# Weight sums of the up projection made in DRAM by accumulating DMA, and fifteen instead of thirteen pairs with seven products

## The chip, the cores and the metric

The kernel runs on one core of a Trainium2 chip. The metric is device time in microseconds: the median of several executions. TensorE (PE) multiplies, VectorE (DVE) and ScalarE (ACT) do elementwise work, GpSimd (POOL) does a few selects and issues the accumulating DMAs, SyncE (SP) issues the plain DMAs. Each engine runs its own instructions strictly in order; between engines there are semaphores. All DMAs run on 16 DMA engines.

## What is computed

One layer of an encoder on 512 tokens with 1024 channels, in float32: three token mixers on one normalised input (a forgetting attention, a gated delta rule, a stick-breaking attention), merged by gates and one output projection; then attention into 256 memory tokens; then a gated MLP. The change concerns the first matrix of the MLP, `w_up` (1024 x 5632):

```
x = x + mixed @ w_out
x = x + memory_cross_attention(rmsnorm(x, norm_xq), rmsnorm(mem, norm_mem), ...)

def conv_ffn(h, w_up, conv_w, conv_b, w_down):
    u = causal_dwconv(h @ w_up, conv_w) + conv_b
    a, b = jnp.split(u, 2, axis=-1)
    return (jax.nn.silu(a) * b) @ w_down

x = x + conv_ffn(rmsnorm(x, norm_ffn), w_up, ffn_conv, ffn_conv_b, w_down)
```

## The kernel before

**Units and splits.** All weights lie in DRAM as units of 128 x 1024 float32 (512 KB), in the order in which they are used. SP loads a unit into one of three buffers `wraw` (`load_unit`, L176). Each number is then split into a high part `whi`, rounded by ScalarE to TensorE's fast float32 format, and a low part `wlo`, the difference, by VectorE (`split_unit`, L181). Both have two buffers. A product of 128 x 512 takes three matmuls for each block of 128 channels: high x high, high x low, low x high (`mm3`, L208). A load is issued when VectorE has done with the unit three before it.

**The low part by DMA.** In the MLP most units get the low part in another way (`split_adding`, L288): ScalarE writes the negative of the rounded number into `alo`, and an accumulating DMA, issued by GpSimd, adds the unit from DRAM to it.

**Pairs.** The MLP has 22 pairs: unit 2m gives 128 columns of `a`, unit 2m + 1 the matching 128 of `b`. A plain pair multiplies both with all 512 tokens, 48 matmuls of 512 columns. A pair in `SEVEN` is made by Strassen's scheme in Winograd's form (`seven`, L297): the weights of the pair are a 2 x 2 array of blocks (a11, a12 in the first unit, a21, a22 in the second), the input another (channel half by token half), and seven products of half width take the place of eight. That is 84 matmuls of 256 columns. The sums of weight blocks s1 to s4 are made by VectorE (L305, L306, L314, L315) from the loaded units and split like units; the sums of input blocks, the token forms t14 and t23, are made once, behind pair 4 (`token_forms`, L1084). a1 and a22 get their low parts by accumulating DMA. Pairs 0 to 6, 15 and 21 are plain. The results lie in three PSUM banks px, py, pz, and five half-width operations of VectorE put them together. After each pair `gated` (L1111) applies the convolution and the gate.

**Stages and order.** The three mixers run first, in the order of the string `ORDER` (L30). Of its steps S3 projects the last stick-breaking head, s3 is that head's attention (its selects are GpSimd's last work for a long time), A, B, C are the gate projections, a, b, c the mixers' output projections, whose units appear as woa, wob, woc. Then come eight units of `wout` (wo0 to wo7) with four of the memory keys (mk) among them, the cross attention, the MLP's pairs, and the down projection. Inside this program order a scheduler fixes each engine's instruction order when the kernel is built; what it set ahead of time can be listed. The memory tokens are loaded as four tiles `mem_sb` (L374) when the mixing stage's buffers are free, and turned into `memh` and `meml` for the key projections.

Of the kernel before, what the change touches and what calls it, by code (L numbers as in the profile page):

```python
# [9 lines left out]
F32 = mybir.dt.float32  # L10
# [3 lines left out]
ALU = mybir.AluOpType  # L14
# [21 lines left out]
LOADS = (0, 1, 3, 2, 4, 5, 6, 7, 8, 9, 10)  # L36
# [45 lines left out]
def build(nc, tc, ctx, x_t, mem_t, w, cols_d, const_d, unit_d, out_t, dbg=None):  # L82
# [9 lines left out]
    def tiles_of(which, tag, bufs, shape=(T,)):  # L92
# [25 lines left out]
    spilled = ctx.enter_context(tc.tile_pool(name="spill", bufs=1, space=bass.MemoryType.DRAM)).tile(  # L118
        [P, KC, T], F32, tag="x3", name="x3_spill")

    def dense_ps(name):
        return pd.tile([P, T], F32, tag="d", name=name)
# [48 lines left out]
    ones_r = cp.tile([P, P], F32R, tag="ones_r", name="ones_r")  # L171


    last_mm = []

    def load_unit(u):  # L176
        raw = wp.tile([P, 1024], F32, tag="wraw", name=f"wraw{u}", bufs=WB[0])
        nc.sync.dma_start(raw, w[u])
        return raw

    def split_unit(u):  # L181
# [70 lines left out]
    def two(t):  # L252
        return t.rearrange("p (f n) -> p f n", f=2)

    def half_product(ps, unit, xs, behind=None):


        wh, wl = unit
        with ExitStack() as order:
            if behind is not None:  # L260
                order.enter_context(tc.issue_after(behind.ins))
            new = behind is None
            first = PE.matmul(ps, wh[:, block(0)], xs[0][0], start=new, stop=False, skip_group_check=not new)
            for i, (xh, xl) in enumerate(xs):
                if i:
                    PE.matmul(ps, wh[:, block(i)], xh, start=False, stop=False, skip_group_check=not new)  # L266
                PE.matmul(ps, wh[:, block(i)], xl, start=False, stop=False, skip_group_check=not new)  # L267
            for i, (xh, _) in enumerate(xs):
                PE.matmul(ps, wl[:, block(i)], xh, start=False, stop=i == 3, skip_group_check=not new)  # L269
        return first  # L270
# [17 lines left out]
    def split_adding(u, src, cols, name):  # L288

        lo = ahead(f"alo{name}", F32R)[:, :cols.stop - cols.start]  # L290
        hi = wp.tile([P, 1024], F32R, tag="whi", name=f"whi{name}", bufs=WB[1])[:, :cols.stop - cols.start]
        S.activation(lo, src, AF.Copy, scale=-1.0)  # L292
        G.dma_start(lo, w[u, :, cols], accum_op=ALU.add)  # L293
        S.activation(hi, src, AF.Copy)  # L294
        return hi, lo

    def seven(u, name, xs, forms, sums, outs, rest):  # L297


        a1, a2 = load_unit(u), load_unit(u + 1)  # L300
        (a11, a12), (a21, a22) = [(t[:, :T], t[:, T:]) for t in (a1, a2)]

        h1, l1 = split_adding(u, a1, slice(0, 2 * T), f"{u}")
        s1, s2, f12 = sums("12")
# [3 lines left out]
        if ADD_A22:  # L308
            h2, l2 = split_adding(u + 1, a22, slice(T, 2 * T), f"{u + 1}")
        else:  # L310
            h2, l2 = (wp.tile([P, 1024], F32R, tag=t, name=f"{t}{u + 1}", bufs=b) for t, b in (("whi", WB[1]), ("wlo", WB[2])))
            split_blocks(a22, h2[:, :T], l2[:, :T])
        s3, s4, f34 = sums("34")
# [5 lines left out]
        half_product(px[:, RIGHT], w5, forms[1], first)  # L319
        v = rest(f"v{name}")  # L320
        S.activation(v, px, AF.Copy)
        first_y = half_product(py[:, LEFT], (h2[:, :T], l2[:, :T]), forms[4])
        half_product(pz[:, LEFT], w6, forms[2])
        half_product(px[:, LEFT], (h1[:, T:], l1[:, T:]), halves_of(xs, 1, LEFT), first)
        half_product(py[:, RIGHT], w7, forms[3], first_y)
        half_product(px[:, RIGHT], w3, halves_of(xs, 1, RIGHT), first)
        u0, u1 = outs()
        V.tensor_tensor(u0[:, RIGHT], pz[:, LEFT], v[:, LEFT], ALU.add)
        V.tensor_tensor(u1[:, RIGHT], py[:, RIGHT], u0[:, RIGHT], ALU.add)
        V.scalar_tensor_tensor(u1[:, LEFT], py[:, LEFT], -1.0, u1[:, RIGHT], ALU.mult, ALU.add)  # L330
        V.tensor_tensor(u1[:, RIGHT], u1[:, RIGHT], v[:, RIGHT], ALU.add)
        V.tensor_tensor(u0[:, RIGHT], px[:, RIGHT], u0[:, RIGHT], ALU.add)
        S.activation(u0[:, LEFT], px[:, LEFT], AF.Copy)
        return u0, u1

    def rsqrt(ps, name, scale, n=T, work=work):
# [95 lines left out]
    pin = tc.keep_in_program_order  # L432
    xs, sums = [], []

    def add_squares(k):
# [453 lines left out]
    for step in ORDER.split():  # L889
        step, h = step[0], int(step[1:] or 0)  # L890
# [143 lines left out]
    mem_v, qs, pts = [], [], []  # L1034
    for step in CROSS.split():
        {"q": memory_query, "w": memory_weights, "v": lambda h: memory_values()}[step[0]](int(step[1:] or 0))
    ym = []
    for h in range(H):
        ps = dense_ps(f"mo{h}")
# [58 lines left out]
        return forms  # L1098

    def seven_up(m):  # L1100
        def sums(which):
            t = wsum(f"s{which}_{m}")

            def split_sums():
                h, l = split_blocks(t, wsumh(f"sh{which}_{m}", F32R), wsuml(f"sl{which}_{m}", F32R))
                return [(h[:, z], l[:, z]) for z in (slice(0, T), slice(T, 2 * T))]
            return t[:, :T], t[:, T:], split_sums

        return seven(UNITS["up"] + 2 * m, str(m), xn, t_forms, sums, lambda: (uwork(f"u{m}"), uwork(f"u{m + NF}")), uwork)

    def gated(m, us):  # L1111
        ab = []
# [12 lines left out]
    def up_product(m, z, x):  # L1125
        ps = (misc_ps if z else dense_ps)(f"up{m + NF * z}")
        u = UNITS["up"] + 2 * m + z
        if z in ADD_PLAIN and m > FORMS:
            unit = split_adding(u, load_unit(u), slice(0, 2 * T), f"{u}")
# [292 lines left out]
```

## Time and profile before

| | |
|---|---|
| median of 3 runs | 1046.45 us (1043.86 to 1046.69) |
| profiled execution, its own time | 1044.74 us |
| span of its profile, first to last instruction | 1043.0 us |
| granted TensorE clock | 1.00 |
| DMA, bytes | 115.06 MB, 110 GB/s on average |

The profile covers one execution. In its rows times count from the start of the span; PE is TensorE's matmuls, PEld its weight loads, PEclk the clock granted to it, and L numbers are lines of the kernel before. The DMA engines' load in forty equal slices of 26 us:

```profile
PEclk9999999999999999999999999999999999999999
DMA  6323221111211111222434323142777788732441
GB/s 235 101 81 101 76 67 61 72 61 63 80 61 62 59 43 61 81 81 81 153 123 127 122 86 119 43 158 96 188 179 185 178 194 191 173 101 103 161 143 61
```

Each digit of the second row is the busy share in tenths. It is low in the mixing stage (slices 3 to 20) and high in the pair stage (slices 29 to 35), where the accumulating DMAs run.

### The profile page before, as it was taken

Reading aid. Unit: us, or ns where it says so; the run is one execution under the profiler, and the core shown is the slowest. Engines: PE = TensorE matmul, PEld = TensorE weight load, DVE = VectorE, ACT = ScalarE, POOL = GpSimd, SP = SyncE. Lnnn points to the kernel's source line nnn. Section 1 sums busy time; section 2 is a strip of 40 time slices with the busy share of each in tenths; the row PEclk is TensorE's granted clock in tenths of the full one; section 3 lists DMA queues with packets and bytes.
Section 4 is the critical chain, followed back from the end, with each engine's and each line's share of the span. In section 5 each row is a group of like instructions: output and inputs, shape, how many; then the busy total and the mean of one; then the engine's idle time right before and its main releaser. Section 6 shows DMA issues by size and latency. Waiting matters only on the chain.

```text
span 1043.0 us, 14582 instructions
## 1 busy us (share of the span) xinstructions
PE 1029.4 (99%) x5529; PEld 873.1 (84%) x5529; DVE 748.8 (72%) x1262; ACT 602.8 (58%) x986; POOL 58.1 (6%) x116
## 2 busy tenths in 40 slices
PE   9999999999999999999999999999999999999998
PEld 7778888778888888788887888778889999989997
DVE  6697768788455443457657757679889988999873
ACT  6376757646242644654545657655677777855431
POOL 0000000101010000000000000000111111100000
PEclk9999999999999999999999999999999999999999
DMA  6323221111211111222434323142777788732441
GB/s 235 101 81 101 76 67 61 72 61 63 80 61 62 59 43 61 81 81 81 153 123 127 122 86 119 43 158 96 188 179 185 178 194 191 173 101 103 161 143 61
DMA packets 34342, 115.06 MB, mean 110 GB/s; under 512 B 3936, under 2 KB 4192, under 8 KB 33760
## 3 DMA queue, kind: packets, MB, share of 16 engines
q1 hardware_dynamic: 29088, 99.45, 28.3%
q0 software_dynamic: 4896, 14.42, 8.4%
q8 instruction: 43, 0.70, 0.3%
q10 hardware_dynamic: 288, 0.27, 0.1%
q14 instruction: 27, 0.22, 0.1%
HBM read 109.93 MB, written 4.19 MB: 109 GB/s over the span
## 4 chain that ended last, share of the span: by engine, by line
PE 94%; DVE 2%; ACT 1%; DMA 1%; issue 1%; SPq 0%; POOL 0%; ACTq 0%; DVEq 0%; POOLq 0%
PE dn L1221 8%; PE g L212 4%; PE g L213 4%; PE g L215 4%; PE up L215 3%; PE up L213 3%; PE up L212 3%; PE px L267 2%; PE px L269 2%; PE gk L469 2%; PE px L266 2%; PE dz L1221 2%; PE dx L1221 2%; PE f L212 1%; PE s L213 1%; PE s L215 1%
## 5 line engine op out<-in xcount | busy, mean ns | idle before, releaser
L186 ACT ACTIVATE whi<-wraw 128x1024 fp32r<-128x1024 f32 x117 | 123.8, 1058 | 150.4 <-PE g L213 38.7
L187 DVE TENSOR_TENSOR wlo<-wraw,whi 128x1024 fp32r<-128x1024 f32 x117 | 142.7, 1220 | 42.7 <-ACT whi L186 21.4
L212 PE MATMUL g<-hh,whi 128*128 128x512 f32 x192 | 77.5, 404 | 1.6 <-DVE gate L485 1.6
L213 PE MATMUL g<-hl,whi 128*128 128x512 f32 x192 | 75.8, 395 | 0.0
L293 POOL DMA_DIRECT2D alo<-w x34 | 29.5, 866 | 422.2 <-ACT alo L292 419.8
L215 PE MATMUL g<-hh,wlo 128*128 128x512 f32 x192 | 51.5, 400 | 0.0
L1221 PE MATMUL dn<-room,whi 128*128 128x256 f32 (+1 forms) x176 | 49.6, 333 | 0.0
L1118 DVE SCALAR_TENSOR_TENSOR uc<-u,cols,uc 128x511 f32<-128x511 f32 (+1 forms) x68 | 48.5, 749 | 0.7 <-ACT uc L1116 0.7
L212 PEld LDWEIGHTS g<-hh,whi 128*128 128x128 f32 x192 | 36.2, 188 | 10.8 <-DVE gate L485 1.4
L215 PEld LDWEIGHTS g<-hh,wlo 128*128 128x128 f32 x192 | 35.8, 188 | 8.3 <-issue 0.5
L213 PEld LDWEIGHTS g<-hl,whi 128*128 128x128 f32 x192 | 36.2, 188 | 7.7
L294 ACT ACTIVATE whi<-wraw 128x1024 fp32r<-128x1024 f32 (+1 forms) x34 | 30.3, 892 | 15.9 <-PE py L267 8.8
L485 DVE TENSOR_TENSOR gate<-g,r_x 128x512 f32<-128x512 f32 x24 | 16.4, 688 | 30.8 <-PE g L215 30.8
L292 ACT ACTIVATE alo<-wraw 128x1024 fp32r<-128x1024 f32 (+1 forms) x34 | 30.2, 887 | 13.1 <-DMA wraw<-w 12.1
L274 DVE TENSOR_TENSOR sl<-s,sh 128x1024 fp32r<-128x1024 f32 x26 | 31.8, 1223 | 5.2 <-ACT sh L273 5.1
L1221 PE MATMUL dn<-room,wlo 128*128 128x512 f32 (+1 forms) x128 | 34.0, 352 | 0.0
L1221 PEld LDWEIGHTS dn<-room,whi 128*128 128x128 f32 x176 | 29.8, 188 | 3.4
L212 PE MATMUL up<-xnh,whi 128*128 128x512 f32 x80 | 31.6, 395 | 0.0
L1221 PE MATMUL dn<-hidl,whi 128*128 128x512 f32 x80 | 31.6, 395 | 0.0
L213 PE MATMUL up<-xnl,whi 128*128 128x512 f32 x80 | 31.6, 395 | 0.0
L273 ACT ACTIVATE sh<-s 128x1024 fp32r<-128x1024 f32 x26 | 27.3, 1051 | 5.6 <-PE px L267 3.2
L1116 ACT ACTIVATE uc<-u,cols 128x512 f32<-128x512 f32 x34 | 26.7, 809 | 4.5 <-DVE u L1191 3.6
(991 smaller groups left out, 3094.4 us busy)
## 6 DMA issues: line engine op xcount, KB each, us to landing
wraw<-w SPq DMA_DIRECT2D x166, 512.0 KB, 3.5
alo<-w POOLq DMA_DIRECT2D x21, 512.0 KB, 6.4
alo<-w POOLq DMA_DIRECT2D x13, 256.0 KB, 5.8
x<-x_t SPq DMA_DIRECT2D x8, 256.0 KB, 6.7
xr<-x_t SPq DMA_DIRECT2D x2, 1024.0 KB, 5.9
x_spill<-xr SPq DMA_DIRECT2D x2, 1024.0 KB, 4.3
x<-x_spill SPq DMA_DIRECT2D x8, 256.0 KB, 4.1
mem_sb<-mem_t SPq DMA_DIRECT2D x4, 256.0 KB, 4.7
```

The costliest lines, as they stand in the source:

```text
L186: S.activation(hi, raw, AF.Copy)
L187: V.tensor_tensor(lo, raw, hi.bitcast(F32), ALU.subtract)
L212: PE.matmul(ps, hi[:, b], xh, start=first and i == 0, stop=False)
L213: PE.matmul(ps, hi[:, b], xl, start=False, stop=False)
L215: mm = PE.matmul(ps, lo[:, b], xh, start=False, stop=last and i == len(xs) - 1)
L273: S.activation(hi, src, AF.Copy)
L274: V.tensor_tensor(lo, src, hi.bitcast(F32), ALU.subtract)
L292: S.activation(lo, src, AF.Copy, scale=-1.0)
L293: G.dma_start(lo, w[u, :, cols], accum_op=ALU.add)
L294: S.activation(hi, src, AF.Copy)
L1118: V.scalar_tensor_tensor(c[:, s:], u[:, :T - s], col("ffn_conv", 3 * j + 2 - s), c[:, s:], ALU.mult, ALU.add)
L1221: mm = PE.matmul(ps[:, z], lhs, rhs, start=first is None, stop=last, skip_group_check=True)
```

## The change

The weight sums are no longer made by VectorE in the pair stage. For each pair in `SEVEN` they are made in a DRAM tile `sums` of 128 x 2048, ahead of time, by DMAs alone. SP copies the second unit into its first half and the first unit into its second half, DRAM to DRAM. Then GpSimd issues three accumulating DMAs, each of which reads what the one before it wrote: a11 and a21 are added to a21 and a22, which gives s3 and s1; s1 is added to a11, which gives s2; s2 is added to a12, which gives s4. [...]

The work on one pair is a generator of four steps: two copies, then the three accumulates, one a step. `advance_sums` moves every unfinished pair by one step and starts the next. It is called once after each of fifteen places, `SUMS_AFTER`: eleven steps of the mixing stage from S3 on, and wo0 to wo3. Copies are put in SP's order right behind the last weight load at that place, and accumulates keep their program order on GpSimd.

In the pair stage a pair now loads a1, a22, and the two halves of `sums` (512, 256, 512 and 512 KB). Only a1 still gets its low part by accumulating DMA. `SEVEN` grows from 13 to 15 pairs (6 and 15 are new).

```diff
-ADD_A22 = True
+ADDED = "1"
+SUMS_AFTER = {"S3": 1, "a0": 1, "A1": 1, "a1": 1, "B0": 1, "c0": 1, "C1": 1, "c1": 1, "B1": 1, "b0": 1, "b1": 1, "wo0": 1, "wo1": 1, "wo2": 1, "wo3": 1}
-SEVEN = (7, 8, 9, 10, 11, 12, 13, 14, 16, 17, 18, 19, 20)
+SEVEN = (6, 7, 8, 9, 10, 11, 12, 13, 14, 15, 16, 17, 18, 19, 20)
...
     def sums_of_tokens(e, o, f):
-        V.tensor_tensor(e[:, LEFT], e[:, RIGHT], e[:, LEFT], ALU.subtract)
-        V.tensor_tensor(two(f), two(e), o[:, None, RIGHT].to_broadcast([P, 2, T // 2]), ALU.add)
-        V.tensor_tensor(e[:, RIGHT], f[:, LEFT], o[:, LEFT], ALU.subtract)
+        V.tensor_tensor(f[:, RIGHT], e[:, RIGHT], o[:, RIGHT], ALU.subtract)
+        V.tensor_tensor(f[:, LEFT], f[:, RIGHT], e[:, LEFT], ALU.subtract)
+        V.tensor_tensor(e[:, LEFT], e[:, LEFT], e[:, RIGHT], ALU.subtract)
+        V.tensor_tensor(e[:, RIGHT], f[:, LEFT], o[:, LEFT], ALU.add)
...
+    def sums_of_weights(m):
+        u = UNITS["up"] + 2 * m
+        t = dram.tile([P, 2048], F32, tag=f"sums{m}", name=f"sums{m}")
+        s31, s2, s4 = t[:, :1024], t[:, 1024:1536], t[:, 1536:]
+        summed[m] = t
+        with tc.issue_after(last_load[0]):
+            nc.sync.dma_start(s31, w[u + 1])
+            nc.sync.dma_start(t[:, 1024:], w[u])
+        yield
+        pin(G.dma_start(s31.rearrange("p (a b) -> p a b", a=2), w[u:u + 2, :, :T].rearrange("a p b -> p a b"), accum_op=ALU.add))
+        yield
+        pin(G.dma_start(s2, s31[:, T:], accum_op=ALU.add))
+        yield
+        pin(G.dma_start(s4, s2, accum_op=ALU.add))
+
+    def advance_sums(n):
+        for s in list(steps):
+            if next(s, steps) is steps:
+                steps.remove(s)
+        for m in SEVEN[len(summed):len(summed) + n]:
+            steps.append(sums_of_weights(m))
+            next(steps[-1])
...
-        V.tensor_tensor(s1, a21, a22, ALU.subtract)
-        V.tensor_tensor(s2, a11, s1, ALU.subtract)
-        w5, w6 = f12()
...
-        V.tensor_tensor(s3, a21, a11, ALU.subtract)
-        V.tensor_tensor(s4, a12, s2, ALU.subtract)
-        w7, w3 = f34()
+        h1, l1 = split("1", load(w[u], ring("1")), w[u])
+        hs31, ls31 = split("3", load(sums[:, :1024], lambda: wsum(f"s31_{name}")), sums[:, :1024])
+        h2, l2 = split("2", load(w[u + 1, :, T:], ring("2")), w[u + 1, :, T:])
+        hs24, ls24 = split("4", load(sums[:, 1024:], lambda: wsum(f"s24_{name}")), sums[:, 1024:])
...
+        if name in SUMS_AFTER:
+            advance_sums(SUMS_AFTER[name])
...
+        advance_sums(SUMS_AFTER.get(f"wo{m}", 0))
...
+    advance_sums(len(SEVEN) - len(summed))
+    while steps:
+        advance_sums(0)
```

Three places in the engines' orders. First GpSimd's, from the last select of the mixing stage on (`s` is the stick-breaking head's tile, `alo` a low part of the MLP). Before:

```order
71 L858 AFFINE_SELECT s_3492<-s_3492 128x128
72 L858 AFFINE_SELECT s_3493<-s_3493 128x128
73 L293 DMA alo_6382<-w 128x1024
74 L293 DMA alo_6414<-w 128x1024
75 L293 DMA alo_6457<-w 128x1024
```

and now:

```order
72 L893 AFFINE_SELECT s_3496<-s_3496 128x128
73 L315 DMA sums_3487<-w 128x2x512
74 L317 DMA sums_3487<-sums_3487 128x512
75 L315 DMA sums_3640<-w 128x2x512
76 L319 DMA sums_3487<-sums_3487 128x512
77 L317 DMA sums_3640<-sums_3640 128x512
78 L315 DMA sums_3805<-w 128x2x512
```

All 45 accumulates stand between that select and the first low part of the MLP, with up to three pairs under way at once. Second, SP's order where the wout units are loaded, ahead of the four tiles of the memory tokens (`wraw_4741` is wo0 before, `wraw_4801` now). Before:

```order
91 L178 DMA wraw_4741<-w 128x1024
92 L178 DMA wraw_4779<-w 128x1024
93 L178 DMA wraw_4816<-w 128x1024
94 L178 DMA wraw_4853<-w 128x1024
95 L178 DMA wraw_4904<-w 128x1024
96 L374 DMA mem_sb_4665<-mem_t 128x512
```

and now, from wo1 on:

```order
116 L180 DMA wraw_4845<-w 128x1024
117 L312 DMA sums_4884<-w 128x1024
118 L313 DMA sums_4884<-w 128x1024
119 L180 DMA wraw_4888<-w 128x1024
120 L312 DMA sums_4927<-w 128x1024
121 L313 DMA sums_4927<-w 128x1024
122 L180 DMA wraw_4931<-w 128x1024
123 L180 DMA wraw_4982<-w 128x1024
124 L312 DMA sums_5021<-w 128x1024
125 L313 DMA sums_5021<-w 128x1024
126 L410 DMA mem_sb_4725<-mem_t 128x512
```

Eight copies (two of them, behind wo0, just ahead of these rows) now stand among the same five loads, and the last two directly ahead of the memory tokens. Third, ScalarE's order at that place (`msh` is the mixers' merged output, rounded; `xqh` the normalised residual). Before:

```order
488 L907 ACTIVATE msh_4643<-gate_3662 128x512
489 L204 ACTIVATE memh_4673<-mem_sb_4665,cols 128x256 x2
490 L363 ACTIVATE memq_4697<-mem_sb_4665 128x256
491 L366 ACTIVATE memq_4699<-mem_sb_4665 128x256
492 L204 ACTIVATE memh_4679<-mem_sb_4667,cols 128x256 x2
493 L366 ACTIVATE memq_4702<-mem_sb_4667 128x256
494 L186 ACTIVATE whi_4818<-wraw_4816 128x1024
```

and now:

```order
488 L944 ACTIVATE msh_4703<-gate_3669 128x512
489 L188 ACTIVATE whi_4890<-wraw_4888 128x1024
490 L188 ACTIVATE whi_4933<-wraw_4931 128x1024
491 L206 ACTIVATE xqh_4834<-xr_4721,cols 128x512
492 L206 ACTIVATE memh_4733<-mem_sb_4725,cols 128x256 x2
```

The splits of wo2 and of the first mk unit now come ahead of the first wait for a memory tile.

More of the change, by code (lines that the diff above doesn't have):

```diff
@@ L292, in split_adding @@
+        V.tensor_tensor(f[:, LEFT], f[:, RIGHT], e[:, LEFT], ALU.subtract)
+        V.tensor_tensor(e[:, LEFT], e[:, LEFT], e[:, RIGHT], ALU.subtract)
+        V.tensor_tensor(e[:, RIGHT], f[:, LEFT], o[:, LEFT], ALU.add)
+    def split_adding(src, dram, name):
+        n = src.shape[-1]
+        lo = ahead(f"alo{name}", F32R)[:, :n]
+        hi = wp.tile([P, 1024], F32R, tag="whi", name=f"whi{name}", bufs=WB[1])[:, :n]
         S.activation(lo, src, AF.Copy, scale=-1.0)
-        G.dma_start(lo, w[u, :, cols], accum_op=ALU.add)
+        G.dma_start(lo, dram, accum_op=ALU.add)
@@ L294, in split_adding @@
         S.activation(hi, src, AF.Copy)
         return hi, lo
[L297 to L304, printed above, removed]
-        V.tensor_tensor(s1, a21, a22, ALU.subtract)
-        V.tensor_tensor(s2, a11, s1, ALU.subtract)
-        w5, w6 = f12()
[L308 to L313, printed above, removed]
-        V.tensor_tensor(s3, a21, a11, ALU.subtract)
-        V.tensor_tensor(s4, a12, s2, ALU.subtract)
-        w7, w3 = f34()
+    summed, steps = {}, []
@@ new lines, in advance_sums, with seven, split, load @@
+    def advance_sums(n):
[5 more added lines that the diff above has]
+            next(steps[-1])
+    def seven(u, name, sums, xs, forms, outs, rest):
+        def split(key, src, dram):
+            if key in ADDED:
+                return split_adding(src, dram, f"{name}_{key}")
+            n = src.shape[-1]
+            return split_blocks(src, *((wp.tile([P, 1024], F32R, tag=t, name=f"{t}{name}_{key}", bufs=b) if key in "12" else
+                                        (wsumh if t == "whi" else wsuml)(f"{t}{name}_{key}", F32R))[:, :n]
+                                       for t, b in (("whi", WB[1]), ("wlo", WB[2]))))
+        def load(dram, alloc):
+            t = alloc()[:, :dram.shape[-1]]
+            nc.sync.dma_start(t, dram)
+            return t
+        def ring(key):
+            return lambda: wp.tile([P, 1024], F32, tag="wraw", name=f"wraw{name}_{key}", bufs=WB[0])
+        h1, l1 = split("1", load(w[u], ring("1")), w[u])
+        hs31, ls31 = split("3", load(sums[:, :1024], lambda: wsum(f"s31_{name}")), sums[:, :1024])
+        h2, l2 = split("2", load(w[u + 1, :, T:], ring("2")), w[u + 1, :, T:])
+        hs24, ls24 = split("4", load(sums[:, 1024:], lambda: wsum(f"s24_{name}")), sums[:, 1024:])
@@ L324, in seven @@
         half_product(px[:, LEFT], (h1[:, T:], l1[:, T:]), halves_of(xs, 1, LEFT), first)
-        half_product(py[:, RIGHT], w7, forms[3], first_y)
-        half_product(px[:, RIGHT], w3, halves_of(xs, 1, RIGHT), first)
+        half_product(py[:, LEFT], (h2, l2), forms[4], first_y)
+        half_product(pz[:, LEFT], (hs24[:, :T], ls24[:, :T]), forms[2])
+        half_product(px[:, RIGHT], (hs24[:, T:], ls24[:, T:]), halves_of(xs, 1, RIGHT), first)
         u0, u1 = outs()
+        S.activation(u0[:, LEFT], px[:, LEFT], AF.Copy)
@@ L887, in delta_out @@
         yb.append(split(y, ytile, f"yb{h}"))
-    for step in ORDER.split():
-        step, h = step[0], int(step[1:] or 0)
+    for name in ORDER.split():
+        step, h = name[0], int(name[1:] or 0)
         {"p": prep_head, "F": fox_qkv, "f": fox_head, "S": stick_qkv, "s": stick_head, "n": scan,
@@ L1100, in seven_up @@
     def seven_up(m):
[L1101 to L1109, printed above, removed]
+        return seven(UNITS["up"] + 2 * m, str(m), summed[m], xn, t_forms, lambda: (uwork(f"u{m}"), uwork(f"u{m + NF}")), uwork)
     def gated(m, us):
@@ L1128, in up_product @@
         if z in ADD_PLAIN and m > FORMS:
-            unit = split_adding(u, load_unit(u), slice(0, 2 * T), f"{u}")
+            unit = split_adding(load_unit(u), w[u], f"{u}")
         else:
```

25 lines of the change are left out of this document (10 added, 15 removed).

## The prediction

> **What bounds the kernel now.** I read the busy table first, then the stages, then the chain that ended last.
>
> ```profile
> PE 1029.4 (99%) x5529; PEld 873.1 (84%) x5529; DVE 748.8 (72%) x1262; ACT 602.8 (58%) x986; POOL 58.1 (6%) x116
> PE 94%; DVE 2%; ACT 1%; DMA 1%; issue 1%; SPq 0%; POOL 0%; ACTq 0%; DVEq 0%; POOLq 0%
> core 0: us, PE busy (x) PEld busy (x) DVE busy (x) ACT busy (x) POOL busy (x), PEclk, DMA share, GB/s
> 0.00:453.00 453.00, 446.61 (x2177) 363.85 (x2178) 291.49 (x533) 250.69 (x459) 28.61 (x82) 1.00 0.24 81
> 453.00:558.00 105.00, 105.00 (x452) 84.41 (x451) 68.44 (x92) 52.40 (x67) 0.00 (x0) 1.00 0.32 106
> 558.00:620.00 62.00, 61.21 (x317) 51.59 (x316) 43.66 (x76) 37.58 (x74) 0.00 (x0) 1.00 0.39 127
> 770.00:860.00 90.00, 90.00 (x717) 88.08 (x716) 80.22 (x131) 69.85 (x95) 15.14 (x18) 1.00 0.80 187
> 925.00:1043.00 118.00, 114.09 (x738) 103.49 (x736) 87.19 (x142) 43.17 (x57) 0.00 (x0) 1.00 0.35 116
> ```
>
> TensorE sets the time: 94% of the chain is its own, and it has no gap at all in 453 to 558 us (the end of the mixing stage) or in 770 to 860 us (the pairs made with seven products). The whole span holds 1043.0 - 1029.4 = 13.6 us without a matmul. So work taken from VectorE, ScalarE or GpSimd in the pair stage gives nothing by itself (80.2 of 90 us on VectorE there is not the limit). Only fewer matmuls can gain, and only something that makes TensorE wait can lose. DMA is the resource with room in the mixing stage (share 0.32) and little in the pair stage (0.80). The change moves DMA work into the first.
>
> **The matmuls saved.** The chain gives the length of both kinds of pair:
>
> ```profile
> 854.87 1.87 PE up L215 x8
> 860.46 1.86 PE up L215 x8
> 863.28 0.48 PE px L269 x4
> 873.26 0.47 PE px L269 x4
> ```
>
> One plain product takes 860.46 - 854.87 = 5.59 us, a plain pair 11.18. From the first px product of one pair of seven to that of the next it is 873.26 - 863.28 = 9.98 us. Two pairs change kind (6 and 15): 2 x 1.20 = **-2.4 us**, all of it on the path. The new scheme has the same 84 half-width matmuls in a pair, so the thirteen old pairs gain nothing on TensorE.
>
> Pair 6 now needs the token forms one plain pair (11.2 us) earlier than pair 7 did.
>
> ```profile
> 760.48 0.69 DVE L1095 TENSOR_TENSOR t14l<-xn,t14h 128x512 fp32r<-128x512 f32 x1
> 772.52 0.28 PE L263 MATMUL px<-t14h,sh 128*128 128x256 f32 x1
> ```
>
> The last form ended at 761.2 and was wanted at 772.5. Wanted 11.2 us earlier, at 761.3, it is just in time. VectorE loses two weight sums of 0.69 ahead of it, but the last forms now stand behind the first bias operations of pair 5. I take **+1 us**, between 0 and +3. The weight sums (4 x 0.69 us a pair) and the accumulating DMA of a22 are hidden behind 9.98 us of TensorE in each pair, so their going counts 0. What replaces them, two more sum loads and one more split of 512 columns, is hidden there too, and would cost only if the stage's DMA share of 0.80 went over 1. A pair's loads go from 1.0 to 1.75 MiB and its accumulates from 0.75 to 0.5, nearly a wash by the prices below.
>
> **The DMA added.** Fifteen times: two copies of 512 KB from DRAM to DRAM on SP's queue, right behind a weight load, and accumulates of 512, 256 and 256 KB on GpSimd's queue. When can they run?
>
> ```profile
> 452.63 0.29 POOL L858 TENSOR_SCALAR_AFFINE_SELECT s<-s 128x128 f32<-128x128 f32 x1 [1.32 <-ACT s L857]
> 736.63 1.01 POOL L293 DMA_DIRECT2D alo<-w  x1 [283.71 <-ACT alo L292]
> L178 SPq DMA_DIRECT2D wraw<-w x18: 327/327/328, 457.5 to 556.5; - x18
> ```
>
> GpSimd's last select is at 452.6 us and its next work is at 736.6. The accumulates stand behind that select in its program, so they start at 453, with six pairs of copies already made, and run without a pause as long as copies are there. They have 284 us, which is enough. But SP issues its last nine pairs of copies among the 18 weight loads of 457 to 556 us, at the same time. The prices:
>
> ```profile
> q1 hardware_dynamic: 29088, 99.45, 28.3%
> q0 software_dynamic: 4896, 14.42, 8.4%
> wraw<-w SPq DMA_DIRECT2D x166, 512.0 KB, 3.5
> x_spill<-xr SPq DMA_DIRECT2D x2, 1024.0 KB, 4.3
> DMA to landing us min/median/max: 3.3/4.2/7.6
> ```
>
> SP's queue held all 16 engines for 0.283 x 1043 / 99.45 = 2.97 us per MB, so 1.56 us for a load and 3.1 us for a pair of copies (1.05 MB). The accumulating queue held them for 0.084 x 1043 / 14.42 = 6.1 us per MB. Sums of 1.05 MB cost 6.4 us a pair, 96 us for fifteen, 2.1 us for each of the 45 accumulates. The trace has no copy and no accumulate whose target is DRAM. A copy's price lies between that of its reading side alone (3.1 us a pair) and reading and then writing (twice that); a write of 1 MB landed in 4.3 us, no slower than reads, so I take 3.1. An accumulate lies between 2.1 us (by bytes) and 3.3 (0.084 x 1043 x 16 / 4896 = 0.286 us a packet, 186 packets each over 16 engines); I take bytes. Could either be cheaper? Lower ends of half these prices are possible, and then nothing below happens.
>
> The last row is the 37 weight loads of 735 to 925 us, where one or two accumulates are in flight: they land after 3.3 us when alone and up to 7.6 when not, that is up to 4.2 us later, two turns of 2.1. So a load isn't passed ahead of an accumulate. I take it that the two queues take turns, one DMA each. The Trainium skill, "DMA: Bandwidth & Descriptors", section "Queues, rings and completion order", says the same: each engine goes round the queue rows that have work and drains a packet of some 9 to 17 descriptors from one before it switches. By that rule the sum is the one that follows; with no such turns it would be the second rival's. No row here has both queues deep at once.
>
> Now the stretch of 105 us. What SP moves there today takes 0.32 x 105 = 33.6 us. Nine pairs of copies add 28. The 38 DMAs of SP (18 loads, 18 copies, 2 of xr) each let one accumulate go first: 38 x 2.1 = 80. That is 142 us. How late may a load be?
>
> ```profile
> 534.09 0.33 SPq L178 DMA_DIRECT2D wraw<-w  x1
> 554.43 0.40 PE L212 MATMUL wo<-msh,whi 128*128 128x512 f32 x1
> ```
>
> The load of the first wout unit is issued at 534.1 and its first matmul is at 554.4: 20.3 us, less 1.3 for the split and 3.5 for a landing alone, leaves 15.5. TensorE thus waits 142 - 105 - 15.5 = **+22 us**, spread over the wob and wout units. TensorE, ScalarE and VectorE all run in order, so a late unit delays everything behind it.
>
> Behind the last copies stand the four loads of mem_sb:
>
> ```profile
> 558.52 4.33 DMA mem_sb<-mem_t
> 566.60 0.50 PE L212 MATMUL wo<-msh,whi 128*128 128x512 f32 x1 [0.79 <-ACT whi L186]
> 572.45 0.12 PE mk L212
> ```
>
> Today they are on the chain and cost 0.8 us, because a weight split waits behind memh on ScalarE. The new order puts two splits ahead of memh, so that goes (**-0.8**), and mem_sb is due only some 1.5 us before mk, at 571. But with the queue as full as above, wo3's load lands at its latest, about 575. Behind it come two copies and the first mem_sb: 3.1 + 0.8 + 3 x 2.1 = 10 us, landing at 585. That is **+14 us** more before mk.
>
> Sum: 1044.7 (the profiled execution's own time, 1.7 below the median of 1046.45) - 2.4 + 1 + 22 - 0.8 + 14 = **1078.5 us**.
>
> By the Trainium skill, the same page, section "Latency and other measured facts", copies between HBM tensors run at 207 to 214 GB/s, so a pair of copies would take an estimated 5.1 us and not 3.1; the nine pairs add 18 us and the sum would be 1096. No run here shows it yet.
>
> **Rivals.**
> 1. *No queue builds up* (the gaining side). If accumulates are served only as they arrive, two in flight against up to eight of SP's, or if they cost half, then 33.6 + 28 + about 45 = 107 us fits the 105 plus 15.5. Time: 1044.7 - 2.4 - 0.8 + 0 to 2 = 1041.5 to 1043.5. For it: in the pair stage the share is 0.80 and TensorE has no gap. Against it: there SP mostly has one load in flight, here a load stands behind two copies.
> 2. *The accumulates are dear*: 3.3 us each gives 38 x 1.2 = 46 us more, 1124; dear copies 28 more.
> 3. *Token forms late, nothing else*: the split of the forms behind pair 5's bias operations costs 3 us; 1045 to 1046, no change that can be told. It decides only if the first rival holds.
> 4. *Sums late on GpSimd*: if the 45 accumulates last beyond 736, pair 5's low parts wait behind them. With 96 us of work, and 142 us for both queues, they end near 640; only the dear prices together reach 736.
>
> **How the numbers follow.** Queue builds up, 1050 to 1125: 0.60. Dearer than 1125: 0.07. No queue: 0.33, of which 0.13 goes to the gain in full and 0.20 to a time of 1042 to 1049, because the best sum (-2.4 - 0.8) is just the 0.3% (3 us) that a measurement can tell from no change. So slower 0.67, same 0.20, faster 0.13. The range takes in the no-queue case and the dear accumulates: 1041 to 1125. The likeliest case alone spans 1050 to 1125.
>
> **What would show it.** Right: TensorE idle of some 35 us between 505 and 600, with waits of ScalarE's weight split on "DMA wraw<-w" and of memh on mem_sb; weight loads there landing after 15 us or more; DMA share near 1 from 470 on; pairs 6 and 15 taking 10 us each. Wrong: loads landing within 15 us and a full TensorE through 453 to 620 (then rival 1), or a gap near 760 (rival 3), or a first wait of GpSimd's split DMA on the sums (rival 4). What would make it wrong is above all the turn-taking, which I read from loads that met one or two accumulates, and prices of DRAM targets that the trace doesn't hold.

## The result, and the profile after

| | before | after |
|---|---|---|
| median of 4 runs each, on one chip | 1045.15 us (1043.48 to 1046.69) | 1073.01 us (1070.9 to 1076.39) |
| after / before, 95% interval | | 1.0270 (1.0236 to 1.0303): slower |
| profiled execution, its span | 1044.74, 1043.0 us | 1072.99, 1071.3 us |

The changed kernel is 28 us slower. Its page first: the busy time, and the chain that ended last by engine.

```profile
PE 1035.6 (97%) x5601; PEld 880.2 (82%) x5601; DVE 738.4 (69%) x1243; ACT 595.8 (56%) x979; POOL 88.4 (8%) x146
...
PE 78%; DMA 11%; ACT 5%; DVE 4%; issue 2%; ACTq 0%; SPq 0%; POOL 0%; DVEq 0%; POOLq 0%
```

The chain was 94% TensorE and 1% DMA; now it is 78% TensorE and 11% DMA. TensorE stands still for 1071.3 - 1035.6 = 35.7 us, before 13.6. Its waits, longest first (total us, times, longest), in 540 to 700 us and behind 700 us:

```profile
PE mk L214 <- ACT memh L206: 8.2, 2, 7.5
PE wo L214 <- ACT whi L188: 7.0, 1, 7.0
PE px L265 <- ACT v L357: 7.1, 7, 3.4
```

The first two are new and lie where the prediction looked. The third is new too and lies in the pair stage, where it saw nothing. To see what each costs, the same matmuls are found in both timelines: the first of wo, mk, mq, of the first pair of seven, and of the last pair (its first up product). After:

```profile
554.56 0.40 PE L214 MATMUL wo<-msh,whi 128*128 128x512 f32 x1
564.56 0.80 PE L214 MATMUL wo<-msh,whi 128*128 128x512 f32 x1 [7.03 <-ACT whi L188]
587.59 0.58 PE L214 MATMUL mk<-memh,whi 128*128 128x256 f32 x1 [7.54 <-ACT memh L206]
632.96 0.39 PE L214 MATMUL mq<-xqh,whi 128*128 128x512 f32 x1
779.56 0.29 PE L265 MATMUL px<-xnh,whi 128*128 128x256 f32 x1
940.59 0.50 PE L214 MATMUL up<-xnh,whi 128*128 128x512 f32 x1
```

And before, where mk began at 572.29 and wo at 554.43:

```profile
613.25 0.39 PE L212 MATMUL mq<-xqh,whi 128*128 128x512 f32 x1
691.28 0.39 PE L212 MATMUL up<-xfh,whi 128*128 128x512 f32 x1
771.08 0.29 PE L263 MATMUL px<-xnh,whi 128*128 128x256 f32 x1
912.10 0.39 PE L212 MATMUL up<-xnh,whi 128*128 128x512 f32 x1
```

| stretch | before, us | after, us | difference |
|---|---|---|---|
| start to wo | 554.43 | 554.56 | +0.1 |
| wo to mk | 17.86 | 33.03 | +15.2 |
| mk to mq | 40.96 | 45.37 | +4.4 |
| mq to up of pair 0 (710.94 after) | 78.03 | 77.98 | 0.0 |
| pairs 0 to 5 (before without its plain pair 6) | 79.80 - 11.18 = 68.62 | 68.62 | 0.0 |
| pairs 6 to 20 (before with pair 6) | 11.18 + 141.02 = 152.20 | 161.03 | +8.8 |
| last pair to the end | 130.9 | 130.7 | -0.2 |

So 19.6 us were lost between wo and mq, and 8.8 in pairs that were to gain 2.4. The first loss by stages (TensorE busy, TensorE's weight loads, VectorE, ScalarE, GpSimd, granted clock, DMA share, GB/s):

```profile
453.00:505.00 52.00, 52.00 (x224) 41.80 (x223) 32.23 (x43) 29.81 (x38) 12.03 (x13) 1.00 0.89 195
505.00:558.00 53.00, 52.53 (x226) 41.94 (x224) 33.70 (x46) 20.50 (x26) 9.45 (x10) 1.00 1.04 268
558.00:580.00 22.00, 15.44 (x60) 12.20 (x60) 4.95 (x6) 4.71 (x6) 2.94 (x4) 0.84 0.98 256
580.00:620.00 40.00, 31.77 (x168) 27.07 (x168) 25.75 (x45) 23.81 (x52) 10.52 (x11) 0.87 0.95 220
```

The DMA engines, which were busy for 0.32 of 453 to 558 us, are full. TensorE doesn't feel it until 557 us, because the loads run ahead; then it waits twice, and after each wait it works at a lower clock. Two pieces of the chain say for which loads it waited (start, length):

```profile
542.26 21.08 DMA wraw<-w
...
567.82 19.19 DMA mem_sb<-mem_t
```

The load of the second wout unit took 21.1 us to land and the first of mem_sb 19.2, against 3.6 and 4.3 us before. The two are links of one chain: ahead of mem_sb in SP's order stands the load of wo3, which waits for the buffer of that late unit (its wlo ended at 565.8 us), so mem_sb was also issued 9.3 us later than before (567.8 against 558.5). What GpSimd did meanwhile (its DMA issues, with its idle time before each and what ended it):

```profile
453.31 1.35 POOL L315 DMA_DIRECT2D sums<-w  x1 [0.26 <-issue]
461.67 0.88 POOL L317 DMA_DIRECT2D sums<-sums  x1 [7.01 <-DMA sums<-w]
462.25 1.51 POOL L315 DMA_DIRECT2D sums<-w  x1
466.64 0.84 POOL L319 DMA_DIRECT2D sums<-sums  x1 [2.89 <-DMA sums<-sums]
```

Each accumulate is issued only when the one that it builds on has landed. From 453 to 575 us 25 were issued; the last of 45 came at 652.5.

In the pair stage the chain goes round a loop. Its pieces over one turn:

```profile
867.52 5.61 DMA wraw<-w
...
873.21 0.87 ACT alo L296
...
874.97 0.48 ACT v L357
875.46 0.95 ACT whi L298
...
877.57 0.68 DVE wlo L276
...
878.28 5.63 DMA wraw<-w
```

A load lands, ScalarE splits it (alo), then copies v, for which TensorE waits, then splits on; VectorE's wlo of the half unit a22 gives a buffer back, and only then SP issues the next load: 878.28 - 867.52 = 10.76 us for a turn, and a pair of seven took 161.03 / 15 = 10.74 us.

### The profile page after: what moved, and what is told of

Read it like the earlier page. It is cut to its first block, busy times and chain, and to the rows that moved or that the text cites. A ratio compares the mean times of both kernels' runs of the same rounds, so it can differ in the third digit from the quotient of the medians.

```text
span 1071.3 us, 14881 instructions
## 1 busy us (share of the span) xinstructions
PE 1035.6 (97%) x5601; PEld 880.2 (82%) x5601; DVE 738.4 (69%) x1243; ACT 595.8 (56%) x979; POOL 88.4 (8%) x146
## 4 chain that ended last, share of the span: by engine, by line
PE 78%; DMA 11%; ACT 5%; DVE 4%; issue 2%; ACTq 0%; SPq 0%; POOL 0%; DVEq 0%; POOLq 0%
DMA wraw<-w 10%; PE dn L1254 8%; PE g L214 4%; PE g L215 4%; PE g L217 3%; PE up L217 2%; PE up L215 2%; PE up L214 2%; PE gk L504 2%; DMA mem_sb<-mem_t 2%; PE dz L1254 2%; PE dx L1254 2%; PE f L214 1%; PE s L215 1%; PE s L217 1%
## 5 line engine op out<-in xcount | busy, mean ns | idle before, releaser
L1151 DVE SCALAR_TENSOR_TENSOR uc<-u,cols,uc 128x511 f32<-128x511 f32 (+1 forms) x76 | 55.2, 747 | 13.8 <-ACT uc L1149 13.4
L275 ACT ACTIVATE whi<-s 128x1024 fp32r<-128x1024 f32 x30 | 31.8, 1058 | 34.0 <-PE px L269 34.0
L276 DVE TENSOR_TENSOR wlo<-s,whi 128x1024 fp32r<-128x1024 f32 x30 | 36.7, 1225 | 17.5 <-ACT whi L275 17.5
L269 PE MATMUL px<-xnl,whi 128*128 128x256 f32 x180 | 45.3, 284 | 0.0
L297 POOL DMA_DIRECT2D alo<-w x19 | 16.6, 876 | 266.9 <-ACT alo L296 266.9
L269 PEld LDWEIGHTS px<-xnl,whi 128*128 128x128 f32 x180 | 34.7, 193 | 0.0
L268 PE MATMUL px<-xnh,whi 128*128 128x256 f32 x135 | 34.6, 284 | 0.0
L296 ACT ACTIVATE alo<-wraw 128x1024 fp32r<-128x1024 f32 x19 | 20.1, 1058 | 24.9 <-DMA wraw<-w 24.8
L214 PE MATMUL wo<-msh,whi 128*128 128x512 f32 x64 | 27.0, 426 | 7.0 <-ACT whi L188 7.0
L1254 PE MATMUL dn<-room,wlo 128*128 128x512 f32 (+1 forms) x128 | 33.6, 352 | 0.0
L275 ACT ACTIVATE whi<-wraw 128x512 fp32r<-128x512 f32 (+1 forms) x27 | 19.5, 722 | 24.3 <-PE dn L1254 23.1
```

What stands on the lines that cost most here:

```text
L214: PE.matmul(ps, hi[:, b], xh, start=first and i == 0, stop=False)
L1151: V.scalar_tensor_tensor(c[:, s:], u[:, :T - s], col("ffn_conv", 3 * j + 2 - s), c[:, s:], ALU.mult, ALU.add)
L1254: mm = PE.matmul(ps[:, z], lhs, rhs, start=first is None, stop=last, skip_group_check=True)
```

## The experiments

All are edits of the changed kernel except e4 and e7, which are edits of the kernel before. "wo to mq" runs from the first wo matmul to the first mq one, "15 pairs" from the first px product to the first up product of pair 21, both from each timeline. Ratios are to the kernel before in the same runs (median 1043.87 us for e1 to e4, 1044.33 for e5 to e10; 1045.15 for the changed kernel).

| kernel | median, us | ratio and interval | wo to mq | 15 pairs |
|---|---|---|---|---|
| before | | 1 | 58.82 | |
| changed | 1073.01 | 1.0270 (1.0236 to 1.0303) | 78.40 | 161.03 |
| e1 own buffers | 1061.58 | 1.0163 (1.0140 to 1.0186) | 79.35 | 149.85 |
| e2 copies only | 1050.79 | 1.0073 (1.0058 to 1.0088) | 58.32 | 160.02 |
| e3 copies early | 1056.98 | 1.0133 (1.0117 to 1.0148) | 65.55 | 161.08 |
| e4 fifteen, old scheme | 1058.06 | 1.0139 (1.0124 to 1.0154) | 58.56 | |
| e5 all early | 1045.20 | 1.0003 (0.9994 to 1.0013) | 58.31 | 149.85 |
| e6 e1 and e3 | 1047.94 | 1.0027 (1.0016 to 1.0037) | 63.40 | 149.85 |
| e7 e4, own buffer | 1051.55 | 1.0058 (1.0043 to 1.0073) | 58.05 | |
| e8 wider | 1085.04 | 1.0389 (1.0360 to 1.0417) | 83.39 | 163.14 |
| e9 spread | 1042.07 | 0.9976 (0.9967 to 0.9985) | 58.30 | 149.85 |
| e10 none at wout | 1059.31 | 1.0132 (1.0106 to 1.0158) | 64.43 | 162.58 |

### e1: the half unit gets buffers of its own

```diff
-AHEAD = 4
+AHEAD = 3
...
+    wraw2 = tiles_of("ahead", "wr2", 2, (512,))
...
         def ring(key):
+            if key == "2":
+                return lambda: wraw2(f"wraw{name}_2")
             return lambda: wp.tile([P, 1024], F32, tag="wraw", name=f"wraw{name}_{key}", bufs=WB[0])
```

> The changed kernel, but the half unit a22 of a pair (512 columns) gets two buffers of its own instead of taking turns with the full unit in the three wraw buffers (paid for with one of the four buffers of the accumulating splits). Theory A, a loop through three buffers: the load of pair m+2's full unit can be issued only when the split of pair m's half unit has given its buffer back, it lands 5.6 us later, and its split stands on ScalarE ahead of the copy v that TensorE waits for; the loop takes 10.7 us. Then with own buffers the px waits on v (7.1 us) go, the fifteen pairs take 150 us in place of 161, and the whole 1073 - 11 = 1062 us; the mixing stage stays as it is. Theory B, the transfers of a pair (1.75 MiB of loads and 0.5 MiB of accumulates) are simply too slow: the pairs stay at 10.7 us each and the time at 1071 to 1074.

Measured 1061.58. The stage from 800 to 930 us, of the changed kernel and then of e1:

```profile
800.00:930.00 130.00, 123.28 (x1010) 121.84 (x1009) 100.02 (x157) 89.33 (x123) 11.16 (x13) 0.99 0.78 216
```

```profile
800.00:930.00 130.00, 130.00 (x1096) 130.00 (x1095) 106.56 (x172) 94.39 (x133) 11.35 (x13) 1.00 0.84 224
```

TensorE is full again, with a DMA share that is higher (0.84), and no px wait is left. The fifteen pairs take 149.85 us, 9.99 each. Theory B, that a pair's transfers are too slow as such, falls; the loop through the three buffers is what cost the 11.2 us between 161.03 and 149.85.

### e2: the copies alone

```diff
-        yield
-        pin(G.dma_start(s31.rearrange("p (a b) -> p a b", a=2), w[u:u + 2, :, :T].rearrange("a p b -> p a b"), accum_op=ALU.add))
-        yield
-        pin(G.dma_start(s2, s31[:, T:], accum_op=ALU.add))
-        yield
-        pin(G.dma_start(s4, s2, accum_op=ALU.add))
+        yield
```

> The changed kernel without its 45 accumulates into DRAM; the copies stay (so the sums hold plain weights). Theory, the loads are held up by taking turns with accumulates: the DMA work between 453 and 578 us falls by about 28 x 2.3 = 64 us, the waits for the second wout unit and for mem_sb (14.4 us more than before) go, and with them the 5 us of lowered clock behind them; the first mq product comes within 1 us of 613.3, and the whole takes 1073 - 19.6 = 1053 us, the pair stage unchanged. Rival, the copies hold up the loads, as they stand ahead of them in SP's queue and cost 5 us a pair rather than 3: most of the 20 us stays, 1065 to 1073 us.

Measured 1050.79, and no loss from wo to mq (58.32 us; the first mq product comes at 614.6, 1.3 us later than before, but this execution had lost 1.8 us by 205 us already). From 453 to 575 us of this kernel, the queue of SP, then the weight loads and the copies (count, KB, median us to landing):

```profile
q1 hardware_dynamic: 6471, 23.56, 55.6%
...
wraw<-w SPq DMA_DIRECT2D x20, 512.0 KB, 3.6
sums<-w SPq DMA_DIRECT2D x18, 512.0 KB, 6.2
```

Loads land as fast as before. So copies behind which a load stands don't hurt by themselves, and the rival falls. The same queue in the same 122 us of the kernel before:

```profile
q1 hardware_dynamic: 3747, 13.63, 33.6%
```

The copies thus cost (0.556 - 0.336) x 122 / (23.56 - 13.63) = 2.7 us per MB, 2.8 us for a pair of them. The prediction took 3.1. The estimate of 5.1 us, worked out from the 207 GB/s of the Trainium skill, "DMA: Bandwidth & Descriptors", section "Latency and other measured facts", doesn't hold here. The Trainium skill gives that rate for rows of 16 KiB that lie 512 KiB apart; a unit of these copies has rows of 4 KiB.

### e3: the copies 100 to 300 us earlier

A pair's copies and its accumulates are now started apart; copy_weights issues the copies of the next pair.

```diff
+COPIES_AFTER = "S0 F1 s0 f1 F2 f2 F3 f3 A0 C0 S1 S2 s1 s2 z".split()
...
+        if name in COPIES_AFTER:
+            copy_weights()
         if name in SUMS_AFTER:
             advance_sums(SUMS_AFTER[name])
```

> The changed kernel with all fifteen pairs of copies issued some 100 to 300 us earlier (behind the steps S0 to z, where the DMA engines are busy for 0.1 to 0.2 of the time); the 45 accumulates stand where they stood. Theory, copies and accumulates together overfill the stretch from 453 to 578 us, neither does alone: what is left there is 33.6 us of loads and some 64 to 75 us of accumulates in 105 us, the waits for wout and mem_sb shrink to 0 to 5 us, and the time is 1053 to 1058 us with an unchanged pair stage. Rival, the turns with accumulates do it by themselves: at least 10 of the 20 us stay, 1063 us or more. If the copies hold up earlier loads, TensorE gets gaps between 130 and 450 us that the changed kernel hasn't.

Measured 1056.98. Of 19.6 us between wo and mq 6.7 are left, in one wait and the lower clock behind it:

```profile
PE wo L215 <- ACT whi L189: 5.6, 1, 5.6
```

The time is in the range of the theory, the wait a little over it. It looks like the wait of the changed kernel, but it isn't for a wout load: those issued from 533 to 557 us landed after 5.3 to 9.2 us. The chain shows what it stands on:

```profile
558.37 9.17 DMA mem_sb<-mem_t
...
567.64 0.63 ACT memh L207 x2
...
570.27 0.96 ACT whi L189
```

In e3, as in e6 and e10 below, ScalarE's order is the old one again, with the splits of wout units behind memh. This is the 0.8 us wait of the kernel before, longer by the 4.8 us by which mem_sb lands later (9.17 against 4.33). In e2 one split stands ahead of memh, mem_sb lands after 7.0 us, and the wait at wo is 0.3 us. So "neither does alone" held for the wout loads: copies alone cost nothing, and accumulates alone cost a third of the 19.6 us, but by way of mem_sb and this order. The copies made early cost TensorE nothing where they lie.

### e4 and e7: fifteen pairs by the old scheme

```diff
-SEVEN = (7, 8, 9, 10, 11, 12, 13, 14, 16, 17, 18, 19, 20)
+SEVEN = (6, 7, 8, 9, 10, 11, 12, 13, 14, 15, 16, 17, 18, 19, 20)
```

> The kernel before with one edit: pairs 6 and 15 are made with seven products too, by the old scheme (sums on VectorE). By the terms of the prediction: 2 x 1.20 us of matmuls saved, token forms 0 to 3 us late: 1042 to 1045 us, with 10.0 us for each of the fifteen pairs. Rival, VectorE (9.7 of 10 us busy in the pair stage, with two more pairs of weight sums) becomes the bound: pairs longer than 10.0 us and 1045 us or more.

Measured 1058.06, far from the terms of the prediction. TensorE has gaps, more in the later part:

```profile
760.00:850.00 90.00, 87.54 (x712) 86.18 (x711) 81.33 (x133) 66.24 (x93) 13.78 (x16) 0.98 0.74 170
850.00:930.00 80.00, 72.62 (x568) 69.39 (x567) 70.81 (x119) 59.45 (x86) 11.22 (x13) 1.00 0.69 159
```

VectorE, the rival, was busy for 0.90 and 0.89 of these stretches, less than the expected 9.7 of 10 us. In the kernel before, pair 15 was a plain one between eight and five pairs of seven. e7 adds a buffer for the second unit:

```diff
-        a1, a2 = load_unit(u), load_unit(u + 1)
+        a1, a2 = load_unit(u), wraw2(f"wraw{u + 1}")
+        nc.sync.dma_start(a2, w[u + 1])
```

> e4 (the kernel before with fifteen pairs of seven) with a buffer of its own for each pair's second unit, and three instead of four buffers of the accumulating splits. If e4's 14 us came from loads that were issued too late for want of a buffer: pairs of 10.0 us and 1042 to 1045 us. Rival, VectorE (8.8 of 10 us busy and in order behind the weight sums) or the accumulating splits, of which the old scheme has two a pair, set the pace: 1050 us or more.

Measured 1051.55: the rival, by its second half. The buffer takes back nearly half of the 14 us. TensorE's largest wait in its pair stage (in the profiled execution, which took 1048.57) is then

```profile
PE px L270 <- DMA alo<-w: 4.0, 5, 1.8
```

that is, for the accumulating splits, which had lost one of their four buffers to pay for this one. Whether the old scheme could have fifteen pairs with both wasn't tried, and what VectorE's order adds in e4 stays open. What the two runs show is that turning pairs 6 and 15 can cost more than the 2.4 us of matmuls, where loads and splits don't keep up with ten microseconds a pair.

### e8: the accumulates of a pair further apart

```diff
         yield
+        yield
         pin(G.dma_start(s2, s31[:, T:], accum_op=ALU.add))
         yield
+        yield
         pin(G.dma_start(s4, s2, accum_op=ALU.add))
```

> The changed kernel with the three accumulates of a pair two steps further apart in GpSimd's order, nothing else moved: an accumulate then waits for one that was issued five or six places ahead, not two or three. Theory: in the change it is GpSimd's own wait for the landing of the accumulate before that keeps their number down (25 issued by 575 us, not the 38 that the prediction counted). Then more are issued here (30 or more by 575 us), the loads land later still, and the time is 1076 to 1085 us. Rival, the DMA engines are full anyway and set the number: again 24 to 27 by 575 us and 1071 to 1075 us.

Measured 1085.04, at the end of the range, and 33 accumulates issued by 575 us in place of 25; some 5 us were lost before wo already. Loads from 453 to 575 us in the changed kernel and in e8 (median us to landing last):

```profile
wraw<-w SPq DMA_DIRECT2D x18, 512.0 KB, 11.6
```

```profile
wraw<-w SPq DMA_DIRECT2D x18, 512.0 KB, 16.1
```

So it was GpSimd's wait for each landing that had held the accumulates back, and the rival falls. With more of them in flight the loads came later.

### e10: no copies behind the wout units

```diff
+COPIES_AFTER = "S3 S3 a0 a0 A1 A1 a1 a1 B0 c0 C1 c1 B1 b0 b1".split()
...
+        for _ in range(COPIES_AFTER.count(name)):
+            copy_weights()
```

> The changed kernel with the copies behind wo0 to wo3 (four of fifteen pairs) issued behind S3 to a1, two pairs behind each; accumulates and all else as in the change. The prediction's step: mem_sb is late because it stands behind the last copies in SP's queue. Then the wait of mk for mem_sb (8.2 us) shrinks to 0 to 2 us, with some 3 us of lowered clock behind it, and the wait at wo, which stands on earlier loads, stays or shrinks somewhat: 1058 to 1063 us. Rival, any load issued there is late, because of the accumulates in flight: mk waits 5 us or more, 1067 us or more.

Measured 1059.31. mk no longer waits: mem_sb lands after 7.3 us, though 30 accumulates were issued by 575 us. What is left between wo and mq is 5.6 us, of which 3.8 is one wait at wo, behind memh as in e3. Four of fifteen pairs of copies, those right ahead of mem_sb, thus carried 14 of the 19.6 us. (ScalarE's order went back too; it is through that order that the 3.8 us arise.)

### e6, e5, e9: both repairs, and the accumulates spread

e6 is e1 and e3 together.

> e1 and e3 in one kernel: own buffers, copies early, accumulates where the change put them. If the two losses stand apart, their gains add: 1073 - 11.4 - 15 = 1046.6, so 1045 to 1049 us, of which about 6.6 us is the wait for the second wout unit that the accumulates cause alone. Rival, a pair stage that is reached earlier meets the last accumulates and loses there: 1050 us or more.

Measured 1047.94, with 3.9 us of waiting at wo, again behind memh: the gains nearly add (25.1 us, where e1 gained 11.4 and e3 16.0). e5 also moves accumulates:

```diff
-SUMS_AFTER = {"S3": 1, "a0": 1, "A1": 1, "a1": 1, "B0": 1, "c0": 1, "C1": 1, "c1": 1, "B1": 1, "b0": 1, "b1": 1, "wo0": 1, "wo1": 1, "wo2": 1, "wo3": 1}
+SUMS_AFTER = {"f1": 4, "f2": 1, "f3": 5, "a0": 1, "A1": 1, "a1": 1, "B0": 1, "c0": 1, "C1": 1, "c1": 1}
+COPIES_AFTER = "R F0 f0 p0 p1 S0 p2 p3 F1 s0 f1 F2 f2 F3 f3".split()
```

> The changed kernel with own buffers for the half unit (as in e1), the copies another 50 us earlier (behind the steps R to f3), and the accumulates spread: 9 of them where GpSimd stands idle around 210 to 265 us, 15 between 310 and 353 us, the other 21 from 453 us on. If the losses are only the full stretch of 453 to 578 us and the loop of three buffers, both go and the matmuls saved are left: 1044.7 - 2.4, so 1041 to 1043.5 us, with the first mq product within 1 us of 613.3 and fifteen pairs in 150 us. Rival 1: GpSimd waits for its accumulates ahead of the expansions and selects of the heads, TensorE gets gaps between 210 and 453 us, 1046 us or more. Rival 2: the 21 late accumulates still hold up the loads of wob and wout, a wait of 3 us or more at wo, 1046 us or more.

Measured 1045.20, no change that can be told, and neither in the expected range nor in a rival's. wo to mq and the pairs are as expected; what is lost is lost by rival 1. GpSimd in e5, and the same select in the kernel before:

```profile
357.13 1.48 POOL L317 DMA_DIRECT2D sums<-w  x1
357.87 1.06 POOL L889 TENSOR_SCALAR_AFFINE_SELECT s<-s 128x128 f32<-128x128 f32 x1
```

```profile
353.14 0.29 POOL L846 TENSOR_SCALAR_AFFINE_SELECT s<-s 128x128 f32<-128x128 f32 x1 [43.36 <-DVE s L845]
```

The select waits behind the fifteenth accumulate, and TensorE behind the select (2.1 us, and then a lower clock). e9 has one step of three accumulates fewer there:

```diff
-SUMS_AFTER = {"f1": 4, "f2": 1, "f3": 5, "a0": 1, "A1": 1, "a1": 1, "B0": 1, "c0": 1, "C1": 1, "c1": 1}
+SUMS_AFTER = {"f1": 4, "f2": 1, "f3": 4, "a0": 1, "A1": 1, "a1": 1, "B0": 1, "c0": 1, "C1": 1, "c1": 1, "B1": 1}
```

> e5 with one difference: 12 accumulates in place of 15 between 310 and 353 us, so 24 in place of 21 from 453 us on. In e5 the fifteenth was issued at 357.1 us, and the first select of the next head came at 357.9 in place of 353.1: TensorE stood 2.1 us and reached woa 3.6 us late. With 12 (some 3.2 us each, done by 349) that goes, and 24 late ones still end before the wout units: 1045.2 - 3.6 = 1041.6, so 1041 to 1043 us, faster than before by 0.1 to 0.3%. Rival, the price is the accumulates' traffic anywhere in the heads' stage, not the one select: again 1044 to 1046 us, or a wait of 2 us or more at wo.

Measured 1042.07, 0.24% faster than before (0.9967 to 0.9985), 2.3 us, and the only version here that beats it. Its mixing and pair stages:

```profile
453.00:558.00 105.00, 105.00 (x453) 84.55 (x453) 66.67 (x89) 52.35 (x67) 23.04 (x26) 1.00 0.87 188
558.00:620.00 62.00, 61.74 (x320) 51.98 (x319) 45.40 (x79) 38.23 (x75) 0.00 (x0) 1.00 0.38 128
800.00:930.00 130.00, 130.00 (x1018) 126.42 (x1017) 110.43 (x179) 95.50 (x138) 9.60 (x11) 1.00 0.71 203
```

## Why the prediction came near, and where its steps failed

The forecast was 1078.5 us and the median 1073.0. The sign and the first mechanism, a queue at the wout units and mem_sb, were right. That the size is so near is luck, because two errors cancel: the mixing stage was put at 35 us and cost 19.6, the pair stage at -2.4 and cost +8.8.

- **Matmuls saved, -2.4.** Right as a price: fifteen pairs take 149.85 us in e1, against 152.20 for the same pairs before. But the changed kernel didn't get it, since its pairs last 10.74 us and not 9.98.
- **Token forms, +1.** Nothing: pairs 0 to 5 take 68.62 us in both. (As the weight sums are now made by additions alone, the subtractions lie in these forms and in the combination of the products.)
- **The pair stage counted as a wash.** This is the step that failed outright. What replaces the old sums was to be "hidden there too, and would cost only if the stage's DMA share of 0.80 went over 1": the share was 0.78, and 11.2 us were lost. 7.1 of them are the px waits. Of the other 4 at most 1.7 are the clock, which stood at half from 813.2 to 816.5 us, behind the longest wait of 3.4 us; the rest wasn't taken apart. A share says nothing on when a load may be issued. The full unit of pair m+2 takes the buffer of pair m's half unit, so it is issued when that is split, and e1 shows that two small buffers remove the loss. That loads also land later here (5.6 us round the loop, 3.5 typical before) makes the loop longer than ten microseconds, but no run separates this from the buffers.
- **Queue at wob and wout, +22.** The mechanism holds: weight loads issued from 517 to 566 us landed after 13 to 24 us (forecast: 15 or more), and e2, e3 and e10 show that it takes both: accumulates in flight, and copies ahead of the load. Mis-sized is the number of accumulates, 38. That they "run without a pause as long as copies are there" failed: each waits for the landing of another, and 25 came by 575 us. By bytes and prices the step stands:

```profile
q1 hardware_dynamic: 5226, 20.09, 49.3%
q0 software_dynamic: 4487, 8.44, 46.9%
```

  In the 122 us from 453 us on the accumulates took 0.469 x 122 = 57 us, 2.3 each (2.1 forecast), and SP's queue 60 us (33.6 + 28 forecast for 105 us). The place was wrong as well: wob, which was to share the stall, lost nothing (wo came at 554.56).
- **One DMA each in turn.** With 38 DMAs of SP's and 25 accumulates in the stretch there was no one-to-one turn for each. The turns by packets that the Trainium skill states ("DMA: Bandwidth & Descriptors", "Queues, rings and completion order") aren't contradicted by the landings of e3 (6.7 us, against 3.6 in e2) and of e8 (16.1), but no run here shows the order of single packets. (Without turns, the outcome would have been that of the first rival, no queue, and not of the second, as the prediction has it.)
- **mem_sb, +14.** As a landing it was nearly exact, forecast for 585 and landed at 587.0, but in part by luck: wo3's load, forecast for 575, landed at 582.0, and mem_sb then only 5.0 us behind it, not 10. e10 shows the cause, the copies ahead of it. The error is in the sum. The 14 us were counted from 571, when mk needs mem_sb if nothing was lost before; after 22 us of loss at wo it needs it at 593, and a mem_sb that lands at 585 costs nothing more. So the two terms can't both be paid in full. Measured, mk began 15.3 us later than before, of which 7 us of waiting had been spent at wo; the terms add up to 36. (They also disagreed on the load: 142 us of work from 453 end at 595, not 575.)
- **The 0.8 us wait that goes.** It is gone in the changed kernel, whose order has two splits ahead of memh. In e3, e6 and e10, which have the old order, it is back and longer.
- **What no step held:** the clock behind a wait. wo to mq grew by 19.6 us, and the waits account for 7.03 + 7.54 + 0.63 - 0.79 = 14.4. In the other 5.2 us the matmuls were slower: the clock was at half (0.50) from 560.6 to 567.4 and from 584.5 to 594.7 us, and TensorE worked for 2.84 and 6.42 us of these, which by an estimate from these rows is 4.6 us lost.
- **Rivals.** The first (no queue) needed the two kinds of transfer not to meet: e9 builds that, with e1's buffers, and its 1042.07 us lie within the rival's 1041.5 to 1043.5. Dear accumulates (3.3 us) didn't show. The forms cost nothing. GpSimd issued its last accumulate at 652.5 us, well before 736.

## What to carry to other kernels

Spare DMA time in a stage is room for bytes, not for latency: before moving transfers there, ask which loads stand behind them and how far those run ahead, and place the transfers so that they end before the stage whose loads are just in time (in e9 the last accumulate was issued at 543.6 us, ahead of wo). A stage with DMA share under 1 can still be bound by one load, where a buffer comes free late; follow the chain round one turn, and compare the turn with the stage's period. When two loads of one path are late, count the second from the time at which its user is due after the first wait, not from the old time. And a wait that carries a weight's name can stand on something else that its engine had to do first: follow the chain to its start.

## What the runs showed of the hardware

- An accumulate whose target is DRAM costs the DMA engines 57 / 8.44 = 6.8 us per MB when they are full, a plain copy from DRAM to DRAM 2.7.
- A wait of TensorE costs more than its length. Behind the 7.5 us wait of the changed kernel (up to 587.6) the clock, third from the end of each row, was halved:

```profile
587.00:592.00 5.00, 3.72 (x10) 2.52 (x11) 4.11 (x9) 4.94 (x11) 0.85 (x1) 0.50 0.87 200
592.00:597.00 5.00, 5.00 (x18) 4.03 (x17) 4.15 (x9) 2.48 (x7) 2.01 (x2) 0.73 0.74 193
597.00:602.00 5.00, 5.00 (x36) 4.65 (x36) 3.53 (x5) 3.65 (x6) 0.85 (x1) 1.00 0.85 128
```

  In e5 even the 2.1 us wait was followed by half the clock (0.50) over 359.4 to 362.7 us. The Trainium skill, "TensorE: Matmul & The Clock Gate", section "What's actually happening", gives half the clock after an idle window of some 3.4 us and full clock after as long a busy one. The long wait agrees (half, then full within 10 us). The short one is shorter than that window, and the clock fell all the same; there the run differs from the Trainium skill.
- An accumulating DMA holds GpSimd for 0.8 to 1.5 us to issue it, and a dependent one for the landing of the other: some 3.2 us for each of the fifteen in e5's stretch from 309 to 357 us, with the DMA engines busy for 0.88 of it.
